# RWKV-7 scans: the products of a head pair as 64-row matmuls on [b | k] in place of zero-padded 128-row ones

## The chip, the cores and the metric

One core of a Trainium2 chip runs the whole program. The metric is the device time of one execution in microseconds (us), and the value quoted is the median of three runs.

The engines are named as the profile names them: PE is the matrix engine (a 128x128 array, PEld its weight loads), DVE the vector engine, ACT the scalar engine, POOL the third elementwise engine, and SP the engine from whose queue nearly all transfers (DMAs) are issued. SPq, DVEq and the like are the sequencers of these engines. Each engine takes its instructions in the order of its own program.

## The reference

Two layers of a bidirectional trunk on 512 tokens of width 1024. Layer 0 mixes tokens by windowed attention, layer 1 by RWKV-7, and each layer ends with a convolutional feed-forward block. The part that matters here is the RWKV-7 scan, run for 16 heads of 64 channels forward and backward over the tokens, with the two results added and normalised per head:

```
def step(state, inp):
    r_t, w_t, k_t, v_t, a_t, b_t = inp
    sa = jnp.einsum('bhvk,bhk->bhv', state, a_t)
    state = state * w_t[:, :, None, :] + sa[..., None] * b_t[:, :, None, :] + v_t[..., None] * k_t[:, :, None, :]
    y = jnp.einsum('bhvk,bhk->bhv', state, r_t)
    return state, y
...
y = y_f + y_b
mean = jnp.mean(y, axis=-1, keepdims=True)
var = jnp.mean(jnp.square(y - mean), axis=-1, keepdims=True)
```

## The kernel before, in words

The kernel doesn't step through tokens. It cuts the 512 tokens into 8 chunks of 64 (`NC`), and treats the 16 heads as 8 pairs `ct`. In every 128-partition tile the two heads of a pair, `e` = 0 and 1, lie in the lower and the upper 64 partitions (`er(e)`), and the two directions are `d` = 0 and 1. Per pair there are eight stages, all in `rwkv_scan`:

- `p`, `prep`: loads the scaled a and r (`AR`) and b (`B0`, as a block diagonal whose other half stays zero).
- `l`, `low`: products of b with [a | r] per chunk and direction, copied from PSUM to `LR`; the 32x32 blocks near the diagonal go by DMA to a scratch in DRAM (`ls`, line 952).
- `s`, `solve`: loads those blocks in another layout (`X`, line 1028) and inverts them all at once by 31 levels of back substitution, two DVE operations per level (lines 1042 and 1044). The inverse leaves through four copies and a DMA to `zs`.
- `P`, `products`: products of k with [a | r] (again through a zero-padded diagonal, `B1`), their masks, and the transposes of b, k and a that the later stages read (`BR`, `XA`).
- `I`, `inverses`: loads the inverted blocks (`T32`, `TT`).
- `L`, `level`: joins the 32-blocks to 64-blocks by two rounds of 32 small matmuls (lines 1071, 1079).
- `B`, `batch`: applies the inverse to all chunks at once (line 1113, "b1" below, and line 1121, "b2"), and gives the matrices `MT` and `QT` (lines 1122, 1124).
- `C`, `chain`: the one part that is serial in the chunks. Eight steps, each with matmuls on `MT` (line 1145), `QT` (1156) and on the chunk's own values (1139, 1142), and a new state `st` written half by DVE (1152) and half by ACT (1154). It ends with the normalisation per head on DVE, ACT and POOL (lines 1166 to 1176), a turn on PE (`yT`, line 1180) and the gate (1182, 1184).

`run` loops over the pairs with `K.order = "p2L0l2B0s2C0P1I1"`: iteration i emits prep(i+2), level(i), low(i+2), batch(i), solve(i+2), chain(i), products(i+1) and inverses(i+1). The three last pairs have nothing left to prepare. The order on each engine is then decided by a scheduler that simulates the emitted program, so rows of different stages interleave; tiles of a pool come round, and a stage that writes a tile waits until the pair that had it before has read it for the last time. Pairs 0 to 2 are prepared ahead of the loop, between the projections that make r, k, v and the rest.

Which engine does a copy is decided by a table, `K.eng`: "VC" alternates DVE and ACT by the running number of the copy, "V" is DVE, "G" POOL. All matmuls are in fp32, and the trace records each as two passes, so 16 matmuls appear as x32.

Of the kernel before, what the change touches and what calls it, by code (L numbers as in the profile page):

```python
# [815 lines left out]
def rwkv_scan(K, A, sc, mid):  # L816
# [9 lines left out]
    MID = ("l21", "gc", "ks", "mask", "id2", "t", "gt", "bo")  # L826
    PLACE = {"early": ("lr0", "lr1", "ar0", "ar1", "ar2", "ar3", "b00", "b01", "X0", "Y", "tg", "tv"),
             "ring": ("b10", "b11", "bku", "rt", "ak", "xa0", "br0", "vv", "mt", "qt", "st", "rv", "vn0", "tt0", "Q", "x1", "t32"),
             "more": ("br1",)}
# [94 lines left out]
    def diagonal(t, ct, d, z):  # L924

        for e in range(2):
            nc.sync.dma_start(out=t[er(e), :, er(e ^ z)], in_=sc["bk"][ct, d][er(e), :, z])
        return t

    def pair(c, hf, d, z):  # L930

# [5 lines left out]
        return pv

    def low(ct, c):

# [13 lines left out]

    def products(ct, c):

        c.RT = mk([P, NC, 2, HD], "rt", K.nrt)
# [3 lines left out]
        br0 = R.BRs[ct % 2]
        c.BR = [br0[:, hf] for hf in range(2)]
        c.XA = R.XAs[ct % len(R.XAs)]
        ak = mk([P, NC, 2, HD], "ak", K.nak)
        vs = sc["v"].rearrange("(c p) v -> p c v", p=HD)
        c.VN = R.VNs[ct % K.nvn]
        c.B[1] = [diagonal(R.B1s[(2 * ct + d) % len(R.B1s)], ct, d, 1) for d in range(2)]
        for e in range(2):
            nc.sync.dma_start(out=c.VN[er(1 - e), :, er(e)], in_=vs[:, :, ct * P + e * HD:ct * P + (e + 1) * HD])
        BU = []  # L970
# [539 lines left out]
```

## Time and profile before

| | |
|---|---|
| median of three runs | 1649.09 us (1647.85 to 1654.86) |
| the profiled execution's own time | 1652.26 us |
| its span, first to last instruction | 1650.3 us |
| mean granted PE clock in it | 0.956 |
| PE busy in the span | 1547.9 us (94%) |
| DVE busy | 1107.1 us (67%) |
| ACT busy | 790.3 us (48%) |
| POOL busy | 412.7 us (25%) |

The page cuts the span into 40 slices of 41 us. The loop of `run` fills the stretch from about 905 to 1243 us; before it lie layer 0 and the projections, and after it the output projection and the last feed-forward block, both dense PE work that the change doesn't touch. A busy PE in this profile has modelled ends: inside a chain, records that wait for a state are spread over the stretch, so its share of busy time says less than the gaps and the starts do.

### The profile page before, as it was taken

To read this page: it belongs to the slowest core of one execution; us is meant where nothing else is said; L and a number is where in the kernel's file an instruction comes from. 1 tells how busy PE (TensorE), PEld (TensorE's weight loads), DVE (VectorE), ACT (ScalarE), POOL (GpSimd) and SP (SyncE) were. 2 spreads that over 40 slices of the span, in tenths; PEclk is the share of its full clock that TensorE was granted. 3 is DMA by queue.
4 is the path that set the end of the run, shared out by engine and by line. 5 is a ranking of instruction groups with operands and counts; after the bars stand their busy time and mean duration, and the time that the engine had idled before them with its cause. 6 is when DMAs were issued, how large, how long until landed. Compare 5 with 4: busy or idle time off the path is not lost.

```text
span 1650.3 us, 26410 instructions
## 1 busy us (share of the span) xinstructions
PE 1547.9 (94%) x10140; PEld 1259.7 (76%) x10140; DVE 1107.1 (67%) x2000; ACT 790.3 (48%) x1512; POOL 412.7 (25%) x375
## 2 busy tenths in 40 slices
PE   8989999999999998899966898889989999999999
PEld 7767788888888886677754787778877788888887
DVE  6876448777763349959998876767746677777322
ACT  5576434444432225557636555656653444444211
POOL 2630012223300025435465222222200223322000
PEclk9999999999999999999976888989999999999999
DMA  5200023333333322349558887888663233333331
GB/s 187 79 22 1 26 90 93 99 102 91 102 102 112 105 90 90 99 159 285 175 172 211 203 171 169 189 169 179 141 192 97 77 99 92 100 95 96 105 116 63
DMA packets 185773, 200.01 MB, mean 121 GB/s; under 512 B 117552, under 2 KB 138672, under 8 KB 185648
## 3 DMA queue, kind: packets, MB, share of 16 engines
q1 hardware_dynamic: 185504, 198.32, 43.3%
q8 instruction: 80, 1.31, 0.3%
q14 instruction: 45, 0.37, 0.1%
q10 hardware_dynamic: 144, 0.00, 0.0%
HBM read 154.51 MB, written 35.39 MB: 115 GB/s over the span
## 4 chain that ended last, share of the span: by engine, by line
PE 71%; DVE 16%; ACT 5%; DMA 4%; issue 3%; POOL 1%; SPq 1%; DVEq 0%; ACTq 0%; POOLq 0%
PE mm L104 16%; PE mm L106 16%; PE mm L105 16%; PE mm L387 2%; PE sc L104 2%; DVE Y L1044 2%; PE sc L105 2%; PE sc L106 2%; DVE wlo L71 2%; DVE tv L1042 2%; PE tp L382 2%; DMA ar<-ars 1%; DMA X<-ls 1%; PE sc L367 1%; PE pre L935 1%
## 5 line engine op out<-in xcount | busy, mean ns | idle before, releaser
L68 ACT CAST whi<-wraw 128x1024 fp32r<-128x1024 f32 (+2 forms) x196 | 200.3, 1023 | 265.5 <-PE mm L105 187.9
L104 PE MATMUL mm<-hl,whi 128*128 128x512 f32 x720 | 281.4, 391 | 1.8 <-DVE xT L1347 0.9
L105 PE MATMUL mm<-hl,whi 128*128 128x512 f32 x720 | 281.5, 391 | 0.4 <-DVE hl L92 0.4
L106 PE MATMUL mm<-hl,wlo 128*128 128x512 f32 x720 | 281.6, 391 | 0.1
L71 DVE TENSOR_TENSOR wlo<-wraw,whi 128x1024 fp32r<-128x1024 f32 (+2 forms) x139 | 166.5, 1198 | 171.1 <-ACT whi L68 170.4
L71 POOL TENSOR_TENSOR wlo<-wraw,whi 128x1024 fp32r<-128x1024 f32 x57 | 137.8, 2418 | 403.8 <-ACT whi L68 403.8
L185 DVE SCALAR_TENSOR_TENSOR conv<-upad,par,conv 128x512 f32<-128x512 f32 x88 | 125.6, 1429 | 63.8 <-ACT conv L182 63.8
L104 PEld LDWEIGHTS mm<-hl,whi 128*128 128x128 f32 x720 | 135.8, 189 | 30.9 <-ACT whi L68 1.7
L106 PEld LDWEIGHTS mm<-hl,wlo 128*128 128x128 f32 x720 | 135.9, 189 | 29.6 <-POOL wlo L71 0.9
L105 PEld LDWEIGHTS mm<-hl,whi 128*128 128x128 f32 x720 | 135.7, 189 | 29.4 <-DVE hl L92 1.1
L106 PE MATMUL mm<-gh,wlo 128*128 128x512 f32 x352 | 139.0, 395 | 0.0
L104 PE MATMUL mm<-gh,whi 128*128 128x512 f32 x352 | 139.0, 395 | 0.0
L105 PE MATMUL mm<-gl,whi 128*128 128x512 f32 x352 | 139.0, 395 | 0.0
L97 ACT CAST gh<-gact 128x512 fp32r<-128x512 f32 x44 | 27.3, 621 | 138.3 <-DVE gact L194 138.3
L1042 DVE TENSOR_TENSOR tv<-X,Y 128x126 f32<-128x126 f32 (+22 forms) x248 | 74.3, 299 | 18.5 <-DMA X<-ls 13.0
L182 ACT ACTIVATE conv<-upad,par 128x512 f32<-128x512 f32 x88 | 71.5, 815 | 21.3 <-DVE upad L180 20.9
L1044 DVE TENSOR_TENSOR Y<-Y,tv 128x126 f32<-128x126 f32 (+22 forms) x248 | 77.6, 313 | 5.8
L106 PEld LDWEIGHTS mm<-gh,wlo 128*128 128x128 f32 x352 | 66.1, 188 | 16.1
L105 PEld LDWEIGHTS mm<-gl,whi 128*128 128x128 f32 x352 | 66.1, 188 | 16.0
L104 PEld LDWEIGHTS mm<-gh,whi 128*128 128x128 f32 x352 | 66.1, 188 | 16.0
L187 DVE SCALAR_TENSOR_TENSOR conv<-upad,par,conv 128x512 f32<-128x512 f32 x88 | 70.0, 798 | 3.0
L192 ACT ACTIVATE silu<-conv 128x512 f32<-128x512 f32 x44 | 27.8, 632 | 91.4 <-DVE conv L187 91.3
(357 smaller groups left out, 3291.4 us busy)
## 6 DMA issues: line engine op xcount, KB each, us to landing
wraw<-in_w_up_dram SPq DMA_DIRECT2D x88, 512.0 KB, 3.5
wraw<-in_w_down_dram SPq DMA_DIRECT2D x32, 512.0 KB, 3.5
ars<-tab SPq DMA_DIRECT2D x16, 512.0 KB, 3.3
bks<-tab SPq DMA_DIRECT2D x16, 512.0 KB, 3.2
ar<-ars SPq DMA_DIRECT2D x16, 512.0 KB, 7.1
b<-bks SPq DMA_DIRECT2D x64, 128.0 KB, 3.7
bku<-bks SPq DMA_DIRECT2D x16, 512.0 KB, 6.2
bm<-br SPq DMA_DIRECT2D x28, 256.0 KB, 6.3
```

What stands on the lines that cost most here:

```text
L68: nc.scalar.copy(out=hi, in_=raw)
L71: lo_engine.tensor_tensor(out=lo, in0=raw, in1=hi.bitcast(F32), op=ALU.subtract)
L104: nc.tensor.matmul(ps, lhsT=lhs[0], rhs=rhs[0], start=first, stop=False)
L105: nc.tensor.matmul(ps, lhsT=lhs[0], rhs=rhs[1], start=False, stop=False)
L106: nc.tensor.matmul(ps, lhsT=lhs[1], rhs=rhs[0], start=False, stop=last)
L182: nc.scalar.activation(out=c, in_=u[:, 1:S + 1], func=AF.Identity, scale=K.par[:, cw + 2 * FT + ch:cw + 2 * FT + ch + 1], bias=K.par[:, cb ...
L185: nc.vector.scalar_tensor_tensor(out=c, in0=u[:, 0:S], scalar=K.par[:, cw + ch:cw + ch + 1], in1=c, op0=ALU.mult, op1=ALU.add)
L187: nc.vector.scalar_tensor_tensor(out=c, in0=u[:, 2:S + 2], scalar=K.par[:, cw + 4 * FT + ch:cw + 4 * FT + ch + 1], in1=c, op0=ALU.mult, op ...
L382: nc.tensor.transpose(out=tp[:, j * P:(j + 1) * P], in_=p[:, e, j * P:(j + 1) * P], identity=K.ident)
L387: nc.tensor.matmul(po[e * HD:(e + 1) * HD, n], lhsT=vn[:, n - 1 + j, kv * HD:(kv + 1) * HD], rhs=pT[:, e, j * P:(j + 1) * P], start=n == 0 ...
L1042: en.tensor_tensor(out=tm, in0=X[:, 0:kx, kx:kx + 1].broadcast_to([P, kx, n]), in1=Y[:, kx:kx + 1, m:hi].broadcast_to([P, kx, n]), op=ALU. ...
L1044: en.tensor_tensor(out=Y[:, 0:kx, m:hi], in0=Y[:, 0:kx, m:hi], in1=tm, op=ALU.add)
```

## The change

`low` and `products` no longer use a block diagonal. For each head and chunk one matmul takes [b | k] as 64 rows by 128 columns (`BK`, loaded for both heads, for e = 1 with the two halves swapped) against the 64 rows of `AR`. So `low` now makes all four products at once, in one PSUM bank per head, and masks the whole 128x512 tile into a new tile `BW`: for e = 0 by one DVE multiplication, for e = 1 by an ACT copy and a POOL multiplication in place. `ls` is stored from the masked tile. The tiles `LR`, `l21`, `RT`, `ak`, `BR`, `BM`, `VN`, `B0`, `B1` and their copies, masks, zero fills and loads go away. The transposes of b, k and a, the products with v, and b1 and b2 become 64-row matmuls, two for each one before, and their results leave PSUM in whole 128x512 tiles (bkt, xa and xv on ACT). The loads of `VV` move from `batch` to `products`, into two buffers. `AR` has 6 tiles, `BK` 4 and `BW` 3, of which pair i takes number i mod 3. The two halves of the chain's output are swapped, and `K.begin` and `K.tail` shift when pairs 0 and 1 are prepared.

The core of the diff (whole removed functions are in the listing above):

```diff
+        R.ARs, R.BKs, R.BWs = [], [], []
+        inputs(1)
...
+
+    def inputs(n, bks=True):
+
+        for _ in range(n):
+            for _ in range(2):
+                R.ARs.append(mk([P, 2, NC, HD], f"ar{len(R.ARs)}"))
+                if bks:
+                    R.BKs.append(mk([P, NC, 2, HD], f"bk{len(R.BKs)}"))
+            R.BWs.append(mk([P, NC, 2, 2, 3 * HD], f"bw{len(R.BWs)}"))
...
+        c.AR, c.BK = [], []
         for d in range(2):
             c.AR.append(R.ARs[(2 * ct + d) % len(R.ARs)])
             nc.sync.dma_start(out=c.AR[d], in_=sc["ar"][ct, d])
-            c.B[0].append(diagonal(R.B0s[d], ct, d, 0))
+            c.BK.append(R.BKs[(2 * ct + d) % len(R.BKs)])
+            nc.sync.dma_start(out=c.BK[d][er(0)], in_=sc["bk"][ct, d, er(0)])
+            for z in range(2):
+                nc.sync.dma_start(out=c.BK[d][er(1), :, z], in_=sc["bk"][ct, d, er(1), :, 1 - z])
...
+    def bk(c, d, e, q):
+
+        return c.BK[d][er(e), at(d, q)].rearrange("p z s -> p (z s)")
 
     def low(ct, c):
 
-        c.LR = R.LRs[ct % len(R.LRs)]
-        c.L21 = mk([P, NC, 32], "l21", K.nl21)
+
+        c.BW = R.BWs[ct % len(R.BWs)]
         for hf in range(2):
             hs = slice(4 * hf, 4 * hf + 4)
             for d in range(2):
-                pv = pair(c, hf, d, 0)
-                copy("L", 2 * hf + d, c.LR[:, hs, d], pv)
+                pvs = [bank().rearrange("p (c s) -> p c s", c=4) for _ in range(2)]
+                for i in range(4):
+                    q = 4 * hf + i
+                    for e in range(2):
+                        T.matmul(pvs[e][:, i], lhsT=bk(c, d, e, q), rhs=c.AR[d][er(e), :, at(d, q)], start=True, stop=True)
                 for e in range(2):
-                    copy("l21", 2 * d + e, c.L21[qr(e, d), hs], (pv if K.l21p else c.LR[:, hs, d])[qr(e, d), :, 32 * (1 - d):32 * (2 - d)])
+                    m = R.mask[:, d, e, None, :].broadcast_to([P, 4, P])
+                    w = c.BW[:, hs, d, e, 0:P]
+                    if eng("w", 2 * d + e) is V:
+                        V.tensor_tensor(out=w, in0=pvs[e], in1=m, op=ALU.mult)
+                    else:
+                        C.copy(out=w, in_=pvs[e])
+                        G.tensor_tensor(out=w, in0=w, in1=m, op=ALU.mult)
         for e in range(2):
             for h in range(2):
                 eng("dl", 2 * e + h).dma_start(out=sc["l"][ct, e, h].rearrange("c d i j -> i c d j"),
-                                               in_=c.LR[qr(e, h), :, :, 32 * h:32 * h + 32])
+                                               in_=c.BW[qr(e, h), :, :, e, 32 * h:32 * h + 32])
...
         for d in range(2):
...
+            pvs = [ch(bank()) for _ in range(2)]
+            for q in range(NC):
+                for e in range(2):
+                    T.transpose(out=pvs[e][:, q], in_=bk(c, d, e, q), identity=K.ident[er(e), er(e)])
+            for e in range(2):
+                copy("bkt", 2 * d + e, c.BW[:, :, d, e, P:], pvs[e])
...
+            pa, pv = ch(bank()), ch(bank())
+            for q in range(NC):
                 for e in range(2):
...
+                    T.matmul(pa[er(e), q], lhsT=c.AR[d][er(e), 0, at(d, q)], rhs=K.ident[er(e), er(e)], start=True, stop=True)
                 for e in range(2):
...
+                    T.matmul(pv[er(e), q], lhsT=c.BW[er(1 - e), q, d, e, 0:HD], rhs=c.VV[er(1 - e), q, d, e], start=True, stop=True)
+            copy("xa", d, c.XA[:, :, d, 0:HD], pa)
+            copy("xv", d, c.XA[:, :, d, HD:P], pv)
...
+        X1 = mk([P, NC, 2, HD], "x1")
+        groups = [(hf, d) for hf in range(2) for d in range(2)]
+        for hf, d in groups:
+            hs = slice(4 * hf, 4 * hf + 4)
+            pv = bank("tt", K.ntp).rearrange("p (c s) -> p c s", c=4)
+            for i in range(4):
+                for e in range(2):
+                    T.matmul(pv[er(e), i], lhsT=c.TT[er(e), 4 * hf + i, d], rhs=c.XA[er(e), 4 * hf + i, d], start=True, stop=True)
+            copy("x1", 2 * hf + d, X1[:, hs, d], pv[:, :, 0:HD])
             for e in range(2):
-                copy("x1", n + e, R.X1[er(e), n:n + 2, :, er(e)], pv[er(e), :, :, 0:HD])
-                copy("vv", n + e, c.VV[er(e), n:n + 2, :, e], pv[er(e), :, :, HD:P])
-        for n in range(0, NC, 2):
-            pv = bank("tt", K.ntp).rearrange("p (c d s) -> p c d s", c=2, d=2)
-            for i in range(2):
-                for d in range(2):
-                    T.matmul(pv[:, i, d], lhsT=R.X1[:, n + i, d], rhs=BM[n // 4][:, (n + i) % 4, d], start=True, stop=True)
-            V.tensor_tensor(out=c.MT[:, n:n + 2], in0=pv[:, :, :, 0:HD],
-                            in1=R.id2[:, None, None, :].broadcast_to([P, 2, 2, HD]), op=ALU.add)
-            V.tensor_tensor(out=c.QT[:, n:n + 2], in0=pv[:, :, :, HD:P], in1=c.RT[:, n:n + 2], op=ALU.add)
+                copy("vv", 4 * hf + 2 * d + e, c.VV[er(e), hs, d, e], pv[er(e), :, HD:P])
+        for hf, d in groups:
+            hs = slice(4 * hf, 4 * hf + 4)
+            pv = bank("tt", K.ntp).rearrange("p (c s) -> p c s", c=4)
+            for i in range(4):
+                for e in range(2):
+                    T.matmul(pv[er(e), i], lhsT=X1[er(e), 4 * hf + i, d], rhs=c.BW[er(e), 4 * hf + i, d, e, HD:], start=True, stop=True)
+            V.tensor_tensor(out=c.MT[:, hs, d], in0=pv[:, :, HD:P], in1=R.id2[:, None, :].broadcast_to([P, 4, HD]), op=ALU.add)
+            q = at(d, 4 * hf)
+            V.tensor_tensor(out=c.QT[:, hs, d], in0=pv[:, :, 0:HD], in1=c.AR[d][:, 1, q:q + 4], op=ALU.add)
 
...
-        R.BRs.append(mk([P, 2, 4, 2, 2, P], "br1"))
-        R.BMs = [mk([P, 2, 4, 2, P], f"bm{i}") for i in range(K.nbm)]
+        inputs(1, False)
...
     K.nmt = 1
+    K.nvv = 2
+    K.begin, K.tail = (2,), ("pls", "", "", "")
+    K.eng.update({"w": "VC", "bkt": "C", "bkt/0": "C", "x1": "CV", "xa": "C", "xv": "C"})
```

Two places show how it moves instructions.

DVE, where the loop reaches the solve of a pair. In the rows of before, evictions of other pairs' products (`rt`, `ak`) and of a chain (`st`) lie ahead of the solve (`tv`, `Y`) and between its levels:

```order
L907 COPY rt_9388<-ar3_5957 128x4x64 x2
L981 TENSOR_TENSOR ak_9393<-mm_7448,mask_5024 128x4x64
L1152 TENSOR_SCALAR st_9240<-bank_9227,gc_5023 128x64
L1042 TENSOR_TENSOR tv_9113<-X0_5960,Y_9109 128x31
L1044 TENSOR_TENSOR Y_9109<-Y_9109,tv_9113 128x31
L1042 TENSOR_TENSOR tv_9116<-X0_5960,Y_9109 128x30
L1044 TENSOR_TENSOR Y_9109<-Y_9109,tv_9116 128x30
L981 TENSOR_TENSOR ak_9393<-mm_7449,mask_5024 128x4x64
L1042 TENSOR_TENSOR tv_9119<-X0_5960,Y_9109 128x58
L1044 TENSOR_TENSOR Y_9109<-Y_9109,tv_9119 128x29x2
L981 TENSOR_TENSOR ak_9393<-pre0_5948,mask_5024 128x4x64
L1042 TENSOR_TENSOR tv_9122<-X0_5960,Y_9109 128x56
```

And of the change, at the same place. `t` at line 1140 ends the normalisation of chain(i-1), `Q` belongs to level(i), the four rows of `bw2` are the masks of low(i+2), `x1` is of batch(i), and `tv` at line 1011 is the first operation of solve(i+2):

```order
L1138 SCALAR_TENSOR_TENSOR t_9483<-bank_9466,par_58,bo_9117 128x512
L1140 TENSOR_TENSOR t_9483<-t_9483,gt_9115 128x512
L913 COPY Q_9647<-mm_7314 128x256
L952 TENSOR_TENSOR bw2_7612<-pre0_5948,mask_5024 128x4x128
L952 TENSOR_TENSOR bw2_7612<-mm_7314,mask_5024 128x4x128
L952 TENSOR_TENSOR bw2_7612<-pre0_5948,mask_5024 128x4x128
L952 TENSOR_TENSOR bw2_7612<-mm_7314,mask_5024 128x4x128
L913 COPY x1_9739<-pre1_5949 128x4x64
L913 COPY x1_9739<-mm_7315 128x4x64
L1011 TENSOR_TENSOR tv_9830<-X2_7615,Y_9826 128x31
```

The first operation of the solve now follows directly on the masks that produce its own input. Behind it in the queue stand, five rows on and later, the evictions of b2 (`mt` and `qt`, lines 1079 and 1081), and then all `st` of chain(i). Before, the operations ahead of the solve belonged to other pairs.

PE, at the end of a chain. Before, the small matmuls of `level` (1071, 1079) and the products of `low` (935) stand between the chain's own steps:

```order
L1142 MATMUL bank<-vv,br_7461 64x64 x4
L1071 MATMUL mm<-t_9508,l_8409 32x32 x13
L1145 MATMUL bank<-st,mt 64x64 x2
L1156 MATMUL bank<-st,qt 64x64 x2
L1071 MATMUL mm<-t_9508,l_8409 32x32 x8
L935 MATMUL pre_5948<-ar_5956,b_5950 128x128 x2
L1145 MATMUL bank<-st,mt 64x64 x2
L1156 MATMUL bank<-st,qt 64x64 x2
L1142 MATMUL bank<-vv,br_7461 64x64 x4
L935 MATMUL pre_5948<-ar_5956,b_5950 128x128 x2
L935 MATMUL pre_5949<-ar_5957,b_5951 128x128 x3
L1079 MATMUL mm<-tt_7453,Q 32x32 x6
```

After, at the same place (1136 is `yT`, 983 and 985 the last of products, 1040 and 1048 the two rounds of `level`, 947 the products of `low`, 1069 b1):

```order
L1136 MATMUL bank<-ident,t 64x64 x16
L985 MATMUL pre_5949<-vv,bw_7320 64x64
L983 MATMUL pre_5948<-ident,ar_7318 64x64 x2
L985 MATMUL pre_5949<-vv,bw_7320 64x64 x2
L947 MATMUL mm<-ar_5950,bk_5951 128x128 x8
L1040 MATMUL pre_5948<-t_10216,bw_7320 32x32 x32
L947 MATMUL mm<-ar_5950,bk_5951 128x128 x8
L1048 MATMUL pre_5949<-tt_7321,Q 32x32 x32
L947 MATMUL pre_5948<-ar_5952,bk_5953 128x128 x4
L1069 MATMUL mm<-xa_7323,tt_7321 64x128 x9
L947 MATMUL pre_5949<-ar_5952,bk_5953 128x128 x4
L1069 MATMUL mm<-xa_7323,tt_7321 64x128
```

All of `low`, and both rounds of `level`, now stand behind `yT` of the chain before, and none of them stands between steps of a chain any more.

## Rows read from the trace of the kernel before

**Rows 1.** The page, part 1: busy us (share), instructions.

```profile
PE 1547.9 (94%) x10140; PEld 1259.7 (76%) x10140; DVE 1107.1 (67%) x2000; ACT 790.3 (48%) x1512; POOL 412.7 (25%) x375
```

**Rows 2.** Windows (start:end, us, busy by engine, PE clock, DMA share, GB/s).

```profile
core 0: us, PE busy (x) PEld busy (x) DVE busy (x) ACT busy (x) POOL busy (x), PEclk, DMA share, GB/s
945.00:1200.00 255.00, 230.31 (x3368) 202.17 (x3366) 182.60 (x588) 162.87 (x459) 54.65 (x91) 0.90 0.79 173
...
866.50:907.70 41.20, 25.36 (x112) 20.19 (x111) 33.17 (x68) 25.76 (x56) 21.73 (x26) 0.64 0.89 210
```

**Rows 3.** DVE timeline, the first operation of two solves, five solves apart.

```profile
934.23 0.20 DVE L1042 TENSOR_TENSOR tv<-X,Y 128x31 f32<-128x31 f32 x1 [3.71 <-DMA X<-ls]
...
1151.17 0.21 DVE L1042 TENSOR_TENSOR tv<-X,Y 128x31 f32<-128x31 f32 x1 [2.78 <-DMA X<-ls]
```

**Rows 4.** Waits, 945 to 1200 us (total us, times, longest).

```profile
DVE st L1152 <- PE bank L1145: 29.6, 16, 4.4
...
DVE tv L1042 <- DMA X<-ls: 9.2, 4, 3.0
```

**Rows 5.** DVE by line, 962.3 to 1205.9 us: busy, mean ns, idle before.

```profile
L1044 DVE TENSOR_TENSOR Y<-Y,tv 128x126 f32<-128x126 f32 (+22 forms) x162 | 46.6, 287 | 3.8
...
L1152 DVE TENSOR_SCALAR st<-bank,gc 128x64 f32<-128x64 f32 x42 | 11.7, 278 | 30.6 <-PE bank L1145 30.6
...
L1122 DVE TENSOR_TENSOR mt<-mm,id 128x256 f32<-128x256 f32 x12 | 5.0, 418 | 0.2
...
L1169 DVE TENSOR_TENSOR t<-bank,rv 128x512 f32<-128x512 f32 x7 | 4.8, 683 | 0.0
```

**Rows 6.** DVE timeline: a normalisation's first and last step, a solve's last copies.

```profile
1168.85 0.69 DVE L1166 TENSOR_REDUCE rv<-bank 128x8 f32<-128x512 f32 x1 [0.72 <-PE bank L1156]
...
1174.15 0.69 DVE L1176 TENSOR_TENSOR t<-t,rv 128x512 f32<-128x512 f32 x1 [0.18 <-POOL rv L1175]
...
1178.24 1.21 DVE L907 COPY X<-Y 64x512 f32<-64x512 f32 x2
```

**Rows 7.** PE timeline, 1176 to 1222 us.

```profile
1177.24 1.15 PE L1180 MATMUL bank<-ident,t 64*64 64x64 f32 x32
...
1179.76 1.95 PE L1121 MATMUL pre<-bm,x 128*128 128x128 f32 x16
...
1182.71 2.05 PE L935 MATMUL mm<-ar,b 128*128 128x128 f32 x16
...
1185.37 0.45 PE L1145 MATMUL bank<-st,mt 64*64 64x64 f32 x8
...
1201.46 0.33 PE L1145 MATMUL bank<-st,mt 64*64 64x64 f32 x4
...
1202.98 0.75 PE L1079 MATMUL mm<-tt,Q 32*32 32x32 f32 x64
...
1218.03 0.33 PE L1145 MATMUL bank<-st,mt 64*64 64x64 f32 x4 [0.40 <-DVE st L1152]
```

**Rows 8.** ACT by line, 962.3 to 1205.9 us.

```profile
L1154 ACT ACTIVATE st<-bank,gc 128x64 f32<-128x64 f32 x42 | 13.1, 312 | 26.4 <-DVE st L1152 25.9
...
L905 ACT COPY lr<-mm 128x512 f32<-128x512 f32 x9 | 5.3, 585 | 7.5 <-PE mm L935 3.8 <-issue 3.6
```

**Rows 9.** POOL by line, 742 to 1216 us.

```profile
L762 POOL TENSOR_TENSOR tkd<-tkd,tk 128x512 f32<-128x512 f32 x14 | 19.4, 1384 | 10.3 <-ACT tkd L673 8.6 <-DVE tv L1042 1.6
```

**Rows 10.** The chain that ended last, 1050 to 1063 us (start, us, what).

```profile
1051.26 0.49 SPq L952
1051.79 0.50 SPq L952
1052.33 2.12 DMA ls<-lr
...
1055.10 4.63 DMA X<-ls
...
1059.85 0.20 DVE tv L1042
```

**Rows 11.** The same chain, 1065 to 1085 us.

```profile
1071.21 0.37 ACT br L905
1071.58 0.28 SPq L1094
...
1072.28 8.61 DMA ar<-ars
```

More of the change, by code (lines that the diff above doesn't have):

```diff
@@ L825, in rwkv_scan @@
     pools = {}
[L826 to L829, printed above, removed]
+    MID = ("gc", "ks", "mask", "id2", "t", "gt", "bo")
+    PLACE = {"early": ("bw0", "ar0", "ar1", "bk0", "bk1", "X0", "Y", "tg", "tv"),
+             "ring": ("bw1", "ar2", "ar3", "bk2", "bk3", "xa0", "vv", "mt", "qt", "st", "rv", "tt0", "Q", "x1", "t32"),
+             }
     def er(e):
@@ L961, in products @@
[L961 to L970, printed above, removed]
@@ L993, in products @@
-        for n in range(0, NC, 2):
-            br = c.BR[n // 4][:, n % 4:n % 4 + 2]
-            pv = bank().rearrange("p (c d s) -> p c d s", c=2, d=2)
-            for i in range(2):
-                for d in range(2):
-                    T.transpose(out=pv[:, i, d], in_=BU[d][:, at(d, n + i)].rearrange("p z s -> p (z s)"), identity=K.ident)
-            copy("bkt", 2 * n, br[:, :, :, 0, 0:HD], pv[:, :, :, 0:HD])
-            for z in range(2):
-                copy("bkt", 2 * n + 1 + z, br[er(1 - z), :, :, 1, 0:HD], pv[er(z), :, :, HD:P])
@@ L1002, in products @@
-        for d in range(2):
-            pv = bank().rearrange("p (c s) -> p c s", c=4)
-            for i in range(4):
-                n = at(d, 2 * i)
-                T.transpose(out=pv[:, i], in_=c.AR[d][:, 0, n:n + 2].rearrange("p c s -> p (c s)"), identity=K.ident)
-            for e in range(2):
-                for i in range(2):
-                    copy("xa", 2 * e + i, c.XA[er(e), i::2, d, 0:HD], pv[er(i), :, er(e)])
-        for hf in range(2):
-            pv = bank().rearrange("p (c s) -> p c s", c=4)
-            for i in range(4):
-                n = 4 * hf + i
-                T.matmul(pv[:, i], lhsT=ak[:, n].rearrange("p d s -> p (d s)"), rhs=c.VN[:, n], start=True, stop=True)
-            for e in range(2):
-                for d in range(2):
-                    q = at(d, 4 * hf)
-                    copy("xv", 2 * e + d, c.XA[er(e), q:q + 4, d, HD:P], pv[er(d), :, er(e)])
+        c.XA = R.XAs[ct % len(R.XAs)]
@@ new lines, in products @@
+        c.VV = mk([P, NC, 2, 2, HD], "vv", K.nvv)
+        vs = sc["v"].rearrange("(c p) v -> p c v", p=HD)
+        for e in range(2):
+            for d in range(2):
+                for q in ((0, 4) if d else (0,)):
+                    n = 4 if d else NC
+                    nc.sync.dma_start(out=c.VV[er(1 - e), q:q + n, d, e],
+                                      in_=vs[:, at(d, q):at(d, q) + n, ct * P + e * HD:ct * P + (e + 1) * HD])
+        for d in range(2):
+            pvs = [ch(bank()) for _ in range(2)]
[4 more added lines that the diff above has]
+                copy("bkt", 2 * d + e, c.BW[:, :, d, e, P:], pvs[e])
@@ L1485, in layout @@
     back = np.arange(HD).reshape(2, 32)[:, ::-1].reshape(HD)
-    m = [np.concatenate([s_ < t_, s_ <= t_, s_ <= t_], axis=1),
-         np.concatenate([(s_ > t_)[:, back], s_ >= t_, (s_ >= t_)[back]], axis=1)]
-    m = np.stack(m, axis=1).astype(np.float32)
-    A["rmask"] = f(np.concatenate([m, m], axis=0))
+    one = np.ones((HD, HD), bool)
+    m = [(np.concatenate([one, s_ <= t_], axis=1), np.concatenate([s_ < t_, s_ <= t_], axis=1)),
+         (np.concatenate([one, (s_ >= t_)[back]], axis=1), np.concatenate([(s_ > t_)[:, back], s_ >= t_], axis=1))]
+    m = np.stack([np.stack([np.concatenate([b, k] if e == 0 else [k, b], axis=0) for e in range(2)], axis=1) for b, k in m], axis=1)
+    A["rmask"] = f(m.astype(np.float32))
     return A
```

97 lines of the change are left out of this document (13 added, 84 removed).

## The prediction, made before the changed kernel had run

> **What bounds the kernel now.** I read the page first: PE is busy in 94% of the span [rows 1], which would make a cut in matmul work pay everywhere. Then the windows: in the scan loop PE is still busy 230.31 of 255 us and DVE only 182.60, at a granted clock of 0.90 [rows 2]. But a busy PE has modelled ends, so the third view is the one that sets the time of the loop, the starts of one recurring instruction. The first operation of a solve starts at 934.23 and, five solves on, at 1151.17: 216.94 / 5 = 43.4 us per pair [rows 3]. This **period** is what the change moves; everything outside 905 to 1243 us stays.
>
> What fills 43.4 us? The reader is to see that no engine is waited for long. The waits between 945 and 1200 us are short and spread: DVE waits 9.2 us in all for a solve's input and 29.6 us for chain matmuls [rows 4]. A solve is 62 operations of 287 ns [rows 5], 17.8 us, but the one at 1151.17 ends with its copies at 1179.45 [rows 6], 28.3 us later, because normalisation, `st`, `ak`, `br` and `Q` of other pairs are done between its levels. PE in the same way puts `low` and `level` between chain steps. So several pairs overlap on every engine, and the loop is held by the sum of many things, PE the fullest. For the change I therefore asked not how much work goes away, but which of these overlaps remain.
>
> **The change, part by part.** *Removed.* On PE a pair has 168 records of 128 rows in `low`, the k products, the transposes and v products, b1 and b2; 16 of them take 1.95 to 2.05 us with the last one's tail [rows 7], so about 0.115 us each and 19 us a pair. *Added.* Twice as many 64-row matmuls. If the two heads' halves run side by side, a pair costs: `low` 64 records x 0.056 = 3.6, bkt about 1, xa and xv 128 records at 0.035 to 0.056 (8 chain records of 64x64 take 0.45 with tail, [rows 7]) 4.5 to 7, b1 and b2 3.6 each, together 16 to 19 us. So PE gains 0 to 3 us a pair: little. On DVE the masks are 4 of 0.683 per pair (the nearest 128x512 operation that reads PSUM, [rows 5]) in place of rt, ak and half the br; on ACT many small copies become few large ones at 0.585 [rows 8]. These sums go down a little on every engine, and alone they would give a small gain.
>
> *Moved.* This is the term that decides. Solve(i+2) reads `ls`, which before was stored from an unmasked copy made from `low` between the chain's steps. After, the order of PE puts all of `low` behind `yT`, the turn that ends the normalisation of the chain before, and the order of DVE puts the solve's first operation directly behind the masks of the same `low`. That operation waits for the X load, and DVE does nothing past it: `mt`, `qt` and every `st` of chain(i) stand behind it, and PE's chain stands behind those. So one pass becomes a loop without overlap, from the end of a solve to the start of the next:
>
> 1. End of the solve: copies 1.21 [rows 6], last chain step with `st` 0.278 [rows 5] and 0.312 [rows 8], `qt` matmuls 0.45 [rows 7], handovers: 2.5 us.
> 2. Normalisation, first to last step, 1168.85 to 1174.84 [rows 6]: 6.0 us.
> 3. `yT` 1.15 [rows 7] and a handover: 1.3 us.
> 4. PE from there to the end of `low`. Rest of xa and xv 0.5. Two rounds of `level`, 64 records in 0.75 each [rows 7] plus the evictions that feed the second: 2.0. `low` as ordered: 16 matmuls with the heads alternating, 32 records at half of 0.115, 1.9; then 16 in runs of 4 for one head alone (947 x4 between b1), which can't pair up, 32 x 0.111 = 3.6. B1 between them 2.0. I take 10.0 us.
> 5. The last mask goes ACT then POOL: 0.585 [rows 8] and about 1.4, the POOL product of two 128x512 tiles at 1384 ns [rows 9], 0.2 for handovers: 2.2 us.
> 6. Store to `ls` and load to `X`, from the issue at 1051.26 to the first solve operation at 1059.85 [rows 10]: 8.6 us.
> 7. The solve itself, 62 x (0.287 + 0.02) = 19.0, with the 8 `mt` and `qt` of 0.418 and 5 `st` of 0.278 between its levels [rows 5], 4.7: 23.7 us.
>
> Sum: 2.5 + 6.0 + 1.3 + 10.0 + 2.2 + 8.6 + 23.7 = 54.3 us against 43.4. That is +10.9 for each of 5 periods, **+54 us**.
>
> The rest of the loop. The last solve is shorter than before by 3 to 4 us, since nothing of a later pair stands in it (24.9 with copies for 28.3): -3. From its end to chain(7), before 1179.45 to 1218.03 [rows 6, 7], 38.6 us. After: terms 1 to 3, `level`, b1 and b2 in line, 9.8 + about 10.7 = 20.5, then chain(6), seven steps at about 1.7 = 12 (the chain of before needed 1185.37 to 1201.46, 16 us, with other matmuls in it, [rows 7]), then 20.5 again: 53 us, +14. The start of the loop: the DVE work ahead of the first solves is 9.4 us before and 8 to 9 after, about 0. Fewer transfers (B1, bku, bm and vn go; 8.61 us for an `ar` load issued behind a wait for an ACT copy, [rows 11], becomes shorter): -5. Total +60. Against the profiled execution's own 1652.3 us that is 1712; this execution lies 3.2 us above the median 1649.1, so the forecast is **1709 us**.
>
> Where a cost is unknown. The row pairs: if halves of the array don't run side by side, term 4 grows by 1.9 in `low` and 2 in b1, +4 a period, +20 in the loop and, with all of b1 and b2 twice, +14 in the tail. If they pair even in the runs of one head, it shrinks by 1.8. The POOL mask could take 0.9 to 2.4 us; the X round trip, in a window with fewer transfers, 6.5 to 8.6. The lower bound, with all of these short and part of `level` done during the normalisation, takes 6 us off each period and 6 off the tail: +24, 1673. The upper bound is the clock. In 866.5 to 907.7 us PE had 25.36 us of work in 41.20 and a granted clock of 0.64 [rows 2], which is a mix of 1.2 and 2.4 GHz; after, PE stands idle for some 8 to 12 us around every load of X, so stretches at 1.2 GHz are to be expected. If terms 3 and 4 ran at half speed throughout, 11 us more a period, +55 and +14 in the tail: 1778; in half of the passes, 1745.
>
> One rule bears on the pairing. The chain's matmuls of 64x64 write both halves' results to one bank in different partitions, and 8 records take 0.45 us [rows 7], where 16 of 128 rows take 2.05: no sign of the halves waiting for each other. The Trainium skill, TensorEngine Tiling (Array Packing), Restrictions and Gotchas, says that different row tiles can't access one PSUM bank at the same time and that software must see to it. By it b1 and b2, which put both heads into one bank, would have to run one half after the other; by an estimate from that page b1 and b2 cost 7 us a pair instead of 3.6 and the sum, with 2 more in each period and 14 in the tail, would be 1733. The trace speaks against a cost of that kind, and the forecast keeps the paired price.
>
> **The rivals.** *(a) Faster.* PE is the bound and the moved order hardly matters: the period falls with PE's work by up to 3 us, and with the shorter waits for `ar` and fewer transfers by 2 more; 5 x 3 to 5, the tail 5 to 10, -25 to -40, so 1609 to 1624. For it: 230 of 255 us busy [rows 2]. Against: DVE's own queue, where the solve stands directly behind its own masks, leaves no room for a period under the sum of terms 2 to 7. It decides if the `low` matmuls and their masks come out 11 us earlier than the sum has them, for instance because term 2 runs beside term 4 on the chip. *(b) No change:* half of that overlap; the period stays within 0.5 us of 43.4 and the tail's cost pays for the transfers saved; 1645 to 1655. It needs just that balance. *(c) Worse than forecast:* unpaired rows or the low clock, 1735 to 1778, as above. For it: the clock of 0.64 where PE has gaps; against: in the loop itself it was 0.90 [rows 2].
>
> **How the numbers follow.** The chain of terms as summed, 1673 to 1735: 0.60. (c): 0.18. (a): 0.15. (b) and small changes near it: 0.07. Half a per cent, 8 us, is about what three runs of this kernel can tell from no change (they spread by 7). So slower by over 0.5%: 0.79, within: 0.06, faster: 0.15. A range that leaves out most of (a) and the end of (c) is 1645 to 1765; the likeliest case's own is 1673 to 1735.
>
> **What the profile of the changed kernel would show.** Right: the first `tv` of successive solves 52 to 57 us apart; DVE's wait for `X<-ls` 8 us or more in every pass, some 40 to 60 us in the loop where it was 9.2; no `low` matmul between chain steps; `yT`, `level`, `low` and b1 in one dense run of 10 to 12 us; POOL's mask of about 1.4 us as the last thing before the `ls` store; a PE less busy and a clock not above 0.90. Wrong in the first place: `low` matmuls that run while the normalisation is under way, a DVE that reaches the solve with X already there, or periods of 43 us and less. Wrong in size: a term 4 far from 10 us (pairing, clock), or a tail from the last solve to chain(7) of other than about 53 us.

## The result, and the profile after

| | before, same chip | after |
|---|---|---|
| median | 1648.47 us (4 runs) | 1731.54 us (1728.13 to 1733.91, 4 runs) |
| ratio | | 1.0498, 95% interval 1.046 to 1.0536 |
| profiled execution | 1652.26 us, span 1650.3 | 1730.89 us, span 1729.1 |

Slower, as forecast, but by 83 us where 60 were forecast. The page of the changed kernel, busy time, granted clock by slices of 43 us, and the first operation of the solves:

```profile
PE 1557.9 (90%) x11612; PEld 1265.2 (73%) x11612; DVE 1091.1 (63%) x1933; ACT 698.2 (40%) x1195; POOL 383.7 (22%) x305
...
PEclk9999999999999999999856766677589999999999
...
L1011 DVE TENSOR_TENSOR tv<-X,Y 128x126 f32<-128x126 f32 (+22 forms) x248 | 67.4, 272 | 56.5 <-DMA X<-ls 49.9
```

ACT, DVE and POOL have less to do than in [rows 1], and PE's busy time is nearly the same. What changed lies in the slices of the scans, where the clock falls. The window of the loop, to be held against [rows 2], and the waits between 960 and 1260 us, which hold five solves (total, times, longest):

```profile
945.00:1200.00 255.00, 193.22 (x3652) 169.69 (x3652) 143.10 (x462) 76.24 (x179) 37.24 (x40) 0.70 0.47 102
```

```profile
ACT st L1110 <- DVE st L1108: 125.0, 39, 14.6
...
DVE tv L1011 <- DMA X<-ls: 33.5, 5, 7.8
...
PE mm L976 <- DVE qt L1081: 29.1, 6, 8.9
```

In the same 255 us PE does 37 us less and DVE 39.5 us less, so both wait. DVE's wait for a solve's input, 9.2 us for four solves in [rows 4], is 33.5 for five, and whatever needs the next DVE operation (`st`, and through `qt` the chain on PE) waits with it. One pass of the loop on DVE, with the first operations of the first and the last solve of the five periods around it:

```profile
942.66 0.20 DVE L1011 TENSOR_TENSOR tv<-X,Y 128x31 f32<-128x31 f32 x1 [9.88 <-DMA X<-ls]
...
1099.30 0.20 DVE L1011 TENSOR_TENSOR tv<-X,Y 128x31 f32<-128x31 f32 x1 [7.17 <-DMA X<-ls]
...
1119.77 1.21 DVE L913 COPY X<-Y 64x512 f32<-64x512 f32 x2
...
1124.13 0.69 DVE L1122 TENSOR_REDUCE rv<-bank 128x8 f32<-128x512 f32 x1 [1.56 <-PE bank L1112]
...
1129.16 0.69 DVE L1132 TENSOR_TENSOR t<-t,rv 128x512 f32<-128x512 f32 x1 [1.81 <-POOL rv L1131]
...
1142.44 0.69 DVE L952 TENSOR_TENSOR bw<-pre,mask 128x512 f32<-128x512 f32 x1 [3.29 <-PE pre L947]
...
1155.85 0.21 DVE L1011 TENSOR_TENSOR tv<-X,Y 128x31 f32<-128x31 f32 x1 [7.79 <-DMA X<-ls]
...
1206.33 0.20 DVE L1011 TENSOR_TENSOR tv<-X,Y 128x31 f32<-128x31 f32 x1 [6.63 <-DMA X<-ls]
```

The same pass on PE, from `yT` to the last `low`, and the chain of work behind it (start, length, what):

```profile
1129.90 1.87 PE L1136 MATMUL bank<-ident,t 64*64 64x64 f32 x30 [3.59 <-DVE t L1132]
...
1132.24 2.08 PE L947 MATMUL mm<-ar,bk 64*128 64x128 f32 x16
1134.24 1.07 PE L1040 MATMUL pre<-t,bw 32*32 32x32 f32 x64
1135.25 1.40 PE L947 MATMUL mm<-ar,bk 64*128 64x128 f32 x16
1136.58 0.75 PE L1048 MATMUL pre<-tt,Q 32*32 32x32 f32 x64
1137.27 1.16 PE L947 MATMUL pre<-ar,bk 64*128 64x128 f32 x8
```

```profile
1143.64 1.10 PE pre L947 x8
...
1144.76 0.59 ACT bw L954
...
1145.42 1.27 POOL bw L955
...
1147.06 3.84 DMA ls<-bw
...
1151.47 4.29 DMA X<-ls
...
1155.85 0.22 DVE tv L1011
```

So the loop is the one forecast: solve, end of the chain, normalisation, `yT`, `low`, mask, store, load, solve, with nothing beside it. The mean of five passes is (1206.33 - 942.66) / 5 = 52.7 us, 43.4 before. The tail is measured to the first state that DVE writes in chain(7), the last chain: at 1293.74 in the changed kernel, and before at

```profile
1217.70 0.27 DVE L1152 TENSOR_SCALAR st<-bank,gc 128x64 f32<-128x64 f32 x1
```

Where the 78.8 us of span went:

| stretch | forecast | measured |
|---|---|---|
| to the loop's first solve (934.23 before) | 0 | 942.66: +8.4 |
| five periods | +54 | 263.7 - 216.9 = +46.7 |
| last solve's first `tv` to chain(7)'s first `st` | +11 | 87.4 - 66.5 = +20.9 |
| behind that | -5 | 435.4 - 432.6 = +2.8 |

### The profile page after: what moved, and what is told of

It reads as the page before. It is cut to its first block, busy times and chain, and to the rows that moved or that the text cites. A ratio compares the mean times of both kernels' runs of the same rounds, so it can differ in the third digit from the quotient of the medians.

```text
span 1729.1 us, 28741 instructions
## 1 busy us (share of the span) xinstructions
PE 1557.9 (90%) x11612; PEld 1265.2 (73%) x11612; DVE 1091.1 (63%) x1933; ACT 698.2 (40%) x1195; POOL 383.7 (22%) x305
## 4 chain that ended last, share of the span: by engine, by line
PE 67%; DVE 19%; DMA 5%; issue 4%; ACT 3%; POOL 2%; SPq 1%; DVEq 0%; POOLq 0%; ACTq 0%
PE mm L105 15%; PE mm L104 15%; PE mm L106 15%; DVE tv L1011 3%; DVE Y L1013 3%; DMA X<-ls 2%; PE mm L387 2%; PE sc L105 1%; PE tp L382 1%; PE sc L104 1%; DVE wlo L71 1%; PE sc L106 1%; PE pre L947 1%; PE sc L367 1%; PE mm L947 1%
## 5 line engine op out<-in xcount | busy, mean ns | idle before, releaser
L1011 DVE TENSOR_TENSOR tv<-X,Y 128x126 f32<-128x126 f32 (+22 forms) x248 | 67.4, 272 | 56.5 <-DMA X<-ls 49.9
L182 ACT ACTIVATE conv<-upad,par 128x512 f32<-128x512 f32 x88 | 71.6, 815 | 21.5 <-DVE upad L180 21.3
L1110 ACT ACTIVATE st<-bank,gc 128x64 f32<-128x64 f32 x56 | 17.6, 314 | 148.8 <-DVE st L1108 148.7
L1013 DVE TENSOR_TENSOR Y<-Y,tv 128x126 f32<-128x126 f32 (+22 forms) x248 | 69.4, 280 | 6.9
```

Of the source, the lines that this page charges most:

```text
L182: nc.scalar.activation(out=c, in_=u[:, 1:S + 1], func=AF.Identity, scale=K.par[:, cw + 2 * FT + ch:cw + 2 * FT + ch + 1], bias=K.par[:, cb ...
L1011: en.tensor_tensor(out=tm, in0=X[:, 0:kx, kx:kx + 1].broadcast_to([P, kx, n]), in1=Y[:, kx:kx + 1, m:hi].broadcast_to([P, kx, n]), op=ALU. ...
L1013: en.tensor_tensor(out=Y[:, 0:kx, m:hi], in0=Y[:, 0:kx, m:hi], in1=tm, op=ALU.add)
```

## Experiments

The theory, (S): the time is lost to the serial loop, because DVE's queue puts the solve behind its own masks and everything else behind the solve. Rivals: (W) the doubled number of 64-row matmuls costs it, and (K) the low granted clock does. Ratios are to the kernel before on the same chip, with 95% intervals. "Period" is the distance of the loop's first and last first `tv`, by 5, in the profile.

**Normalisation as a stage of its own, emitted ahead of the next batch.**

```diff
+    def norm(ct, c):
...
+                if x == "B" and i:
+                    stage("N", i - 1)
                 stage(x, i + k)
+        stage("N", KT - 1)
```

> The changed kernel with the normalisation of a chain written as a stage of its own that is emitted one iteration later, behind level and low and ahead of batch; nothing else differs. Theory S (one pass is a serial loop: end of a solve, normalisation, yT, level and low, masks, store and load, next solve): the 5.7 us of normalisation and the 1.9 us of yT leave the stretch ahead of low, so the period falls from 52.7 to 45 to 47 us, the tail gains 2 to 4 more, and the time falls by 30 to 42 us, to 1690 to 1702. Theory K (the loop is slow because PE runs at 1.2 GHz in it): PE stands still as long as before around the load of X, the clock stays near 0.70 in the loop and the time within 10 us of 1731. Theory W (64-row matmuls cost more PE time than the 128-row ones did): same matmuls, same time.

1738.14 us (1727.8 to 1749.68), 1.0502 (1.0444 to 1.0559), period 54.2: no gain. `low` did start before `yT`, but then ran at the lower level of the clock, 1.2 GHz. Two of its runs for one head alone (x8, PE), and the window around all four (the granted clock, 0.50, stands behind the busy times):

```profile
1134.51 2.07 PE L947 MATMUL pre<-ar,bk 64*128 64x128 f32 x8
1137.83 2.07 PE L947 MATMUL pre<-ar,bk 64*128 64x128 f32 x8
```

```profile
1134.00:1148.00 14.00, 14.00 (x132) 12.19 (x124) 2.84 (x5) 3.62 (x9) 3.10 (x3) 0.50 0.29 74
```

They took 1.16 in the changed kernel. The four of them alone give back 3.6 us; the DVE masks also still stood behind the normalisation's last operation. So (K) is real, and eats a part of what (S) frees; how much of it isn't shown.

**The solve behind `qt` on DVE,** by a copy that must read `qt` of the pair two behind, and is then overwritten.

```diff
+        if ct > 1 and hasattr(R.cs[ct - 2], "QT"):
+            V.tensor_copy(out=Y[:, 0], in_=R.cs[ct - 2].QT[:, NC - 1, 1, 0:16])
         G.memset(Y, 0.0)
```

> The changed kernel with one small DVE copy that writes a corner of QT of pair i into the solution tile of solve(i+2) before it is cleared, so that the solve's first operation stands behind the eight mt and qt evictions on DVE. Theory S: these eight (3.3 us) and the first chain step are done while X is still on its way, no longer between the levels; the solve shortens by 3.5 to 5 us a period, so 17 to 25 us in all, to 1706 to 1714. The wait for X on DVE then falls from 6 to 8 us to 3 to 5. Theories K and W: the matmuls and the idle of PE stay, the time within 8 us of 1731.

1700.02 us, 1.0266 (1.024 to 1.0293), period 47.7, and DVE's wait for X 15.3 us in five solves. One row moved in one queue takes the ratio from 1.0498 to 1.0266, more than expected, with no matmul changed.

**All masks on DVE,** none on ACT and POOL.

```diff
+    K.eng["w"] = "V"
```

> The changed kernel with all eight masks of low on DVE (0.69 us each) in place of ACT copy and POOL product for the second head (0.58 and 1.27). Theory S: the last mask before the store ends about 1.2 us earlier, the period falls by 1 to 1.5 us, 5 to 8 us in all, to 1723 to 1727. If DVE were the bound, 4 masks more a pair would cost 2.8 us a period, to 1745. K and W: no change.

1719.27 us, 1.0386 (1.0359 to 1.0413). Period 51.9, and the loop's first solve starts at 933.82 instead of 942.66. In all five runs with the masks on DVE this solve starts at 933.8 to 937.7, in the others of the changed kernel at 940.6 to 944.1. So the +8.4 at the start came from the masks that went through ACT and POOL; in the loop they cost 0.6 to 0.8 us a pass.

**`low` ahead in the order of stages.**

```diff
+    K.order = "p2l2L0B0s2P1C0I1"
```

> The changed kernel with the stages of an iteration emitted as prep, low, level, batch, solve, products, chain, inverses: low ahead of level, products ahead of chain. On PE the products of low then stand between the last chain steps and ahead of yT, and the copies of the transposes ahead of the chain. Theory S: normalisation, yT and both rounds of level leave the way to the solve, 9 to 10 us a period; against that chain steps move behind the solve's levels, up to 8 us. Between 1680 and 1722; low's masks end before yT in the trace. K: clock in the loop stays near 0.70 and the time within 10 us of 1731. W: same matmuls, same time.

1729.45 us, 1.0437 (1.0402 to 1.0473), period 52.9: missed. The chain's steps moved behind the solve and took what the earlier `low` had freed.

**The changed kernel once more,** as a control.

> The changed kernel once more, as the control for the three runs beside it: 4.6 to 5.4% above the kernel before, period near 52.7 us.

1729.99 us, 1.0464 (1.0433 to 1.0494), period 52.5.

**The kernel before, with the loop's dependency alone.** Its 128-row matmuls, masks and loads stay; two tiny copies make `LR` of pair i+2 wait for the gated output `z` of chain(i-1).

```diff
         c.LR = R.LRs[ct % len(R.LRs)]
+        if ct > 2:
+            V.tensor_copy(out=c.LR[:, :, 0, 0:1], in_=ch(R.cs[ct - 3].z)[:, :, 0:1])
+            V.tensor_copy(out=c.LR[:, :, 1, 0:1], in_=ch(R.cs[ct - 3].z)[:, :, 0:1])
...
+        c.z = z
```

> The kernel before with one dependency added: ahead of low(i), from the fourth pair on, two small DVE copies (128x8) write a column of LR from the finished output of chain(i-3), so that the evictions of low can't start before that normalisation, yT and gate have ended. No matmul is changed, all stay 128-row. Theory S: the store to ls, and with it the solve, then comes behind normalisation, yT, low's eviction and the round trip, as in the changed kernel; the period rises from 43.4 to 49 to 55 us, the time by 28 to 58 us, and the wait for X grows to 5 us or more a pass. Theory W (the price is that of the 64-row matmuls and of the new masks): no change beyond the 4 us of the copies. K: slower only as far as the clock falls with it.

1694.47 us, 1.0255 (1.022 to 1.029). The DVE timeline's first operations of two solves, five apart, and the wait for X:

```profile
937.62 0.20 DVE L1045 TENSOR_TENSOR tv<-X,Y 128x31 f32<-128x31 f32 x1 [4.11 <-DMA X<-ls]
...
1182.83 0.20 DVE L1045 TENSOR_TENSOR tv<-X,Y 128x31 f32<-128x31 f32 x1 [3.46 <-DMA X<-ls]
```

```profile
DVE tv L1045 <- DMA X<-ls: 15.2, 5, 4.7
```

The period is 49.0 us with the clock at 0.88 in the loop. One dependency, with the old matmuls and nearly the old clock, gives about half of the loss. For that half (W) isn't needed, and (K) neither.

**Unread matmuls in the wait for X,** to hold the clock up: 32 of 128x64 behind the chain's first products.

```diff
+            for i in range(32 if j == 0 and ct < KT - 1 else 0):
+                T.matmul(c.gn[:, 0:HD], lhsT=K.ident, rhs=c.VV[:, 4 + i % 4, 1, 1], start=True, stop=True)
```

> The changed kernel with 32 matmuls of 128x64 that nobody reads, placed on PE behind the chain's first value products, where PE waits 9 us for mt and qt (which stand on DVE behind the wait for X). They take 3.5 us at 2.4 GHz and 7 at 1.2. Theory K: PE stays busy there, the clock stays at full speed into the chain, and yT, level and low run at 2.4 GHz; the period falls by 2 to 4 us, 10 to 20 us in all. Theory S alone: they lie in a wait, so the time stays within 5 us of the control; the clock may rise in that stretch but falls again in the sparse chain steps.

1788.76 us, 1.082 (1.0787 to 1.0853), period 60.8. As a test of the clock it failed: the added work took 7.4 us where 3.5 were expected, and the scheduler put the chain's second `st` behind the solve's levels. The clock was 0.98 in 1110 to 1130 us and then 0.50, with PE busy 2.56 of 10 us, in 1130 to 1140, so the first 16 records of `low` met the lower level all the same. The next 16 ran at a granted clock of 1.00 (the window in the third row):

```profile
1164.39 2.08 PE L947 MATMUL mm<-ar,bk 64*128 64x128 f32 x16
...
1167.32 1.16 PE L947 MATMUL mm<-ar,bk 64*128 64x128 f32 x16
```

```profile
1167.30:1168.50 1.20, 1.20 (x30) 1.06 (x30) 0.42 (x1) 0.00 (x0) 1.17 (x1) 1.00 0.75 169
```

What the run does show is the price of a chain that stands behind its solve.

**The solve behind `qt`, and the masks on DVE.** Both edits above.

> The second and the third experiment together: the solve's first operation behind mt and qt, and all masks on DVE. Theory S: two different terms of the same loop, so the gains add: 2.3 and 1.1% under the changed kernel give a ratio of 1.015 to 1.02 to the kernel before, with a period of 46 to 47.5 us. If both only removed the same wait, it would stay at 1.025.

1683.87 us, 1.0187 (1.0158 to 1.0215), period 45.8. The two gains add, as expected.

**`level` and `inverses` ahead of the chain,** so that they no longer stand between `yT` and `low`.

```diff
+    K.order = "p2l2B0s2I1L1C0P1"
```

> The changed kernel with inverses and level of pair i+1 emitted ahead of chain(i), where level(i) stood at the head of iteration i before. On PE, low then stands in one run of 32 matmuls with alternating heads behind yT, without the two rounds of level and without the pieces of b1 between. Theory S: term 4 shrinks from 13 us to some 4 at 2.4 GHz or 7 at 1.2, the period from 52.7 to 44 to 47, the last two pairs lose level too; 35 to 55 us less than the changed kernel, a ratio of 1.013 to 1.026 to the kernel before. Theory K: as long as PE idles around X the clock stays near 0.70 and most of this is lost, as in the first experiment: 1.035 or more.

1740.94 us, 1.0539 (1.051 to 1.0568), period 53.7: missed. The stretch from the end of `yT` to the end of `low` did shrink, to about 7 us. But a copy `x1` of the batch now stood behind the solve's first operation on DVE, and b2 on PE waited for it:

```profile
1109.02 1.97 PE L1078 MATMUL pre<-bw,x 64*64 64x128 f32 x16 [7.92 <-DVE Y L1013]
```

The blocking had moved from the chain to the batch. The time is also the one set for (K), 1.035 or more, and the clock was 0.66 in 945 to 1200 us, but the wait in this row is for a queue.

**These three edits together.**

> The edit of the ninth run on top of the eighth (solve behind mt and qt, masks on DVE). Theory S: the gains add, period 38 to 42 us, where DVE's own work of 33 us a pair comes near; a ratio of 0.98 to 1.0 to the kernel before. K: above 1.01.

1680.44 us, 1.0175 (1.0147 to 1.0202), period 44.9, not under 1 as expected. That is the outcome set for (K), above 1.01, and the clock in 945 to 1200 us was 0.71, as in the changed kernel with its 0.70; so this run can't put what is left of the loss down to one of the two theories. The pass from 1072.73 to 1117.46 is the same loop: solve 18.6, end of the chain 2.4, normalisation 5.7, `yT` with the rest of xv 2.3, `low` 5.9, mask 0.65, store, load and handovers 9.2.

**With the normalisation as a stage too.**

> The tenth with the normalisation emitted behind low as in the first experiment. Low then needs no yT ahead of it, but yT's pieces stand between its eights. S: 0 to 4 us a period less than the tenth, if PE is at full clock there; as the first run showed, nothing if it is at 1.2 GHz. Ratio 0.97 to 1.0.

1677.8 us, 1.0153 (1.012 to 1.0186), period 46.2; 0.2% from the run before it, with intervals that overlap.

**Normalisation behind `qt` on DVE,** by a read of `qt` as above, with the three edits.

```diff
-        Q = mk([P, NC, 32], "Q", 2)
+        Q = mk([P, NC, 32], "Q", 1)
...
+        if ct < KT - 1:
+            V.tensor_copy(out=m, in_=R.cs[ct + 1].QT[:, :, 1, 0])
         V.tensor_reduce(out=m, in_=Y, axis=AX.X, op=ALU.add)
...
+                if x == "s" and i:
+                    stage("N", i - 1)
                 stage(x, i + k)
...
+    K.ngt, K.nbo = 2, 2
```

> All edits of the run with three edits (masks on DVE, solve behind qt, level and inverses ahead of the chain), and the normalisation of pair i-1 is made to wait on DVE for the last qt of pair i, so that it runs between the levels of the next solve and no longer between the last chain step and low; it has two buffers for gt and bo to do so. Theory of the serial loop: the terms normalisation 5.7 and yT 2.3 leave the path before low, and part of the normalisation comes back between the solve's levels (about 3 to 5 us on DVE). The loop is then: last step 2.4, low 5.9, mask 0.65, round trip 8.6, solve 18.6 plus 3 to 5, so 39 to 41 us a pair where the three edits had 44.9. Five periods give 20 to 29 us: 1650 to 1665 us, ratio 1.00 to 1.01 to the kernel before. Rival, the clock: a PE that comes from a chain with gaps does low at 1.2 GHz as it did when the normalisation alone was put later, low takes 9 to 10 us, and the period stays at 43 to 45, ratio 1.014 to 1.02. Rival, the queues: the batch's copies or the chain's st come to stand behind something else that waits, and the period rises above 45, ratio 1.02 or more.

1681.63 us, 1.0179 (1.0147 to 1.021), period 45.7: missed. DVE waits only 2.9 us in all for X, and the normalisation runs between the solve's levels, yet the period is no shorter. In the longest of the five passes, from 1116.11 to 1164.30, `low` on PE now waits for a load of `bk`, and on DVE the first masks wait for `low`:

```profile
1147.18 2.55 PE L947 MATMUL pre<-ar,bk 64*128 64x128 f32 x13 [2.05 <-DMA bk<-bks]
```

```profile
1145.12 1.29 DVE L952 TENSOR_TENSOR bw<-mm,mask 128x512 f32<-128x512 f32 x2 [6.16 <-PE mm L947]
...
1150.07 1.29 DVE L952 TENSOR_TENSOR bw<-pre,mask 128x512 f32<-128x512 f32 x2 [3.66 <-PE pre L947]
```

The solve, with the normalisation in it, takes 21.3 us to its copies, xa and xv run to 1143.9 and `low` to 1154.2, and the clock is 0.58 and 0.67 in 1116 to 1139 and 1139 to 1149 us. This pass lost the normalisation and gained a load, products at a lower clock and a longer solve (18.6 in the run with three edits). No version beat the kernel before.

## Why the prediction was right, and where its sum was off

**The mechanism held.** Of the signs that it named, these are in the rows: X waits in every pass, no `low` inside a chain, POOL's mask as the last thing before the store, a clock under 0.90. The wait for X is shorter than the 8 us that it gave (6.0 to 7.8, 33.5 in all), and two of the five periods are under its 52 us. That the order by itself costs time is shown from both sides, for about half of the loss: undoing it in one queue (the solve behind `qt`) gives 2 to 2.3% back (from 1.0464 or 1.0498), making it in the kernel before, with its 128-row matmuls, costs 2.5%. The masks' way through ACT and POOL makes another 0.8 to 1.1%. For the rest, the clock, the runs of `low` for one head alone and the tail are not told apart.

**Term by term,** the pass of 1099.30 to 1155.85, the longest of the five, and the mean of all five:

| term | forecast | this pass | mean |
|---|---|---|---|
| 1 end of the solve | 2.5 | 4.4 | 3.8 |
| 2 normalisation | 6.0 | 5.7 | 5.7 |
| 3 `yT` and handover | 1.3 | 2.0 | 2.0 |
| 4 PE to the end of `low` | 10.0 | 12.9 | 10.9 |
| 5 mask | 2.2 | 2.0 | 2.0 |
| 6 store and load | 8.6 | 9.1 | 8.1 |
| 7 solve | 23.7 | 20.5 | 20.3 |
| sum | 54.3 | 56.6 | 52.7 |

Term 7 was too high: the eight `mt` and `qt` and five `st` are there, but an operation of a level takes 254 ns, not 287 and 20 behind it (DVE by line, 1099.30 to 1119.77 us):

```profile
L1011 DVE TENSOR_TENSOR tv<-X,Y 128x126 f32<-128x126 f32 (+22 forms) x31 | 7.9, 254 | 8.1 <-DMA X<-ls 7.2
```

The mean of before held stretched operations. An update of 128x96 elements takes 0.25 us at 1104.88 in the changed kernel; before, one took 0.78 while POOL worked on `br`:

```profile
1157.29 0.78 DVE L1044 TENSOR_TENSOR Y<-Y,tv 128x96 f32<-128x96 f32 x1
```

```profile
1156.13 1.82 POOL L978 TENSOR_TENSOR br<-lr,mask 64x256 f32<-64x256 f32 x2
```

Between 940 and 1240 us of the kernel before, 50 level operations take over 15% longer than the shortest of their shape, and 48 of them run beside a POOL operation on `br` (lines 978 and 988); in the changed kernel none of the level operations runs beside POOL's masks, and none is stretched.

Terms 1, 3 and 4 were too low. In term 1 two chain steps, not one, are left behind the solve in three of the passes; in the other two it is 2.5, as forecast. In 3 and 4 durations of a full clock were used, and the rows are of both levels: 30 records of `yT` 1.87 where [rows 7] has 32 in 1.15, the first 16 of `low` 2.08 and the next 16, at a granted clock of 0.81, 1.40, where the run with unread matmuls has 1.16 at 1.00, `level` 1.07 and then 0.75. By these rows the lower clock costs 2.2 us in this pass. The errors partly cancel: 54.3 forecast, 52.7 the mean, +46.7 for +54 in the loop.

**The terms that were mis-sized most** lie outside the loop. *The start,* taken as 0 from DVE's work alone: +8.4, shown by the masks-on-DVE run to be the way through ACT and POOL. *The tail,* +20.9 for +11: by the DVE timeline of the changed kernel

```profile
1228.04 0.28 DVE L1108 TENSOR_SCALAR st<-bank,gc 128x64 f32<-128x64 f32 x1
...
1253.84 0.27 DVE L1108 TENSOR_SCALAR st<-bank,gc 128x64 f32<-128x64 f32 x1
...
1262.92 0.69 DVE L1122 TENSOR_REDUCE rv<-bank 128x8 f32<-128x512 f32 x1 [0.83 <-PE bank L1112]
...
1273.35 2.29 DVE L71 TENSOR_TENSOR wlo<-wraw,whi 128x896 fp32r<-128x896 f32 x2 [4.72 <-ACT whi L68]
1275.55 0.75 DVE L1138 SCALAR_TENSOR_TENSOR t<-bank,par,bo 128x512 f32<-128x512 f32 x1
...
1293.74 0.27 DVE L1108 TENSOR_SCALAR st<-bank,gc 128x64 f32<-128x64 f32 x1
```

the last solve took 21.7 (24.9 forecast), then 25.8 to chain(6)'s first `st` at 1253.84 (20.5), 9.1 for the chain (12), and 30.8 for the last turn (20.5). In the first turn the clock was low:

```profile
1231.00:1254.40 23.40, 18.78 (x437) 17.86 (x430) 9.03 (x20) 7.78 (x20) 1.63 (x1) 0.63 0.40 87
```

In the last turn the output projection's `wlo` waits for ACT at the head of DVE's queue, ahead of the `t` that ends `yT`: 6.9 us from the end of the step before to that `t`, 2.1 in the earlier pass. Then that projection's `ol` stands among the eight `mt` and `qt`, which take 8.2 us from first to last (from 1285.61 us) and 3.4 in the turn before. I had laid the chain's terms in line without asking what else would come to stand in the queue. *Fewer transfers* were to give 5 us behind it: +2.8, so none of that is seen there.

**The rivals.** (a), PE as the bound, falls with the 37 us less of PE work in the same window. (c) came out in part: the granted clock is 0.70 in the loop, but the total stays just under that rival's 1735 to 1778. The halves did pair: at a granted clock of 1.00, 16 records of `low` with the heads alternating take 1.16 (the run with unread matmuls), no more than 8 of one head alone. And b1 and b2, 64 records each with both heads in one bank, take 3.7 each, for which the forecast had 3.6; half of b1 in the last experiment, and the window of b1 and b2:

```profile
1155.30 1.91 PE L1071 MATMUL pre<-xa,tt 64*64 64x128 f32 x32
```

```profile
1154.00:1161.50 7.50, 7.50 (x150) 7.21 (x151) 3.78 (x10) 3.46 (x10) 0.00 (x0) 1.00 0.34 61
```

The Trainium skill, TensorEngine Tiling (Array Packing), Restrictions and Gotchas, says that different row tiles can't access one PSUM bank at the same time; no cost of that kind shows in these rows, in which the halves write different partitions of the bank. The 1733 that the prediction worked out by this rule comes nearest to the measured time; that is luck, since the cost that it adds isn't in the rows.

**What stays open:** how much of the 83 us is the clock's. The rows above give 2.2 us of one pass, and the chain and the tail have their part too; the run that should have kept the clock up moved the chain instead. Nor was a version tried that keeps the clock and frees `low` together.

## What to carry to other kernels

When a change lets a producer and its consumer stand next to each other in one in-order queue with a DRAM round trip between them, add up the way round that loop before counting the work saved: here 9.3 us a pass were lost while every elementwise engine had less to do. A wait at the head of DVE's queue can be moved behind work by one read of a few columns (2% here), but three of the further moves (`low` ahead, `level` ahead, the normalisation behind `qt`) put another wait in its place. Ask of every stretch, the start and the tail too, what else the scheduler will put into the queue that waits.

## What the runs showed of the hardware

The clock can stay low under a PE that is busy throughout by the trace: in the run with the normalisation as a stage, 1134 to 1148 us, PE is busy in 14.00 of 14.00 us and the granted clock is 0.50, behind a chain whose matmuls have gaps. What half-height matmuls cost hangs on the order in which the halves are issued: at a granted clock of 1.00, 8 records of 64x128 for one head alone took 1.16 us (the changed kernel) and 16 with the heads alternating 1.16 too (the run with unread matmuls); at 0.50 they took 2.07 and 2.08. At both levels the second head was free. And DVE operations that run beside a POOL operation can take much longer: in the run with `low` ahead two 128x8 steps of the normalisation took 0.65 and 1.09 us beside POOL's masks (at 1142.73 and 1145.53 us), 0.17 each in the changed kernel, where no mask ran beside them. The runs don't show what stretches them.
